# A second norm summed over all partitions, and a copy of half of retention's split outputs, in a hybrid S5 and retention layer

## The chip, the cores and the metric

The kernel runs on one core of one Trainium2 chip. The metric is the device time of one launch in microseconds (us), lower is better. A run is one timed execution; a profiled execution is one that the hardware profiler recorded, with its own time.

## The reference, cut to what matters

One decoder layer for 256 prompt positions and 8 x 8 sample positions, 320 columns together. D is 2048, the feed-forward width 5632.

```python
def rms_norm(x, g):
    y = xf * lax.rsqrt(jnp.mean(xf * xf, axis=-1, keepdims=True) + NORM_EPS)
    return (y * g.astype(jnp.float32)).astype(x.dtype)

def hybrid_layer(...):
    h = rms_norm(x, norm_mix)
    u, q, k, v, g = jnp.split(h @ w_in, [...], axis=-1)
    s5_out, s5_re, s5_im = s5_mixer(u, ...)        # scan, gelu, then y * sigmoid(y @ w_glu + b_glu)
    ...                                            # rotary, chunked retention o, group norm
    ret_out = (jax.nn.silu(g.astype(f32)) * o).astype(x.dtype)
    x = x + jnp.concatenate([s5_out, ret_out], axis=-1) @ w_out
    h2 = rms_norm(x, norm_ffn)                     # the second norm
    gate, up = jnp.split(h2 @ w_ffn_in, 2, axis=-1)
    x = x + (jax.nn.silu(gate) * up) @ w_ffn_out
    return x, s5_re, s5_im, ret_new
```

A final rms_norm follows.

## The kernel before

Everything is kept transposed: features on the 128 partitions, the 320 positions along a row. A matrix product for one block of 128 output features is a chain of products over blocks of 128 input features, into one PSUM buffer of 128x320. Each input block takes three products in fp32r (a 32-bit type of TensorE), because weights and activations are split into a high and a low part (`x = hi + lo`): hi x hi (line L143), hi x the activation's lo (L144), lo x hi (L145).

`wload` brings the weights of eight input blocks (128x1024) at a time: SP issues the transfer into `raw`, ScalarE casts to `hi` (L131), VectorE subtracts to `lo` (L133). Each of the three has a ring of three buffers, so the cast for one load waits until TensorE has done with the load three before it. Behind the first gate output the rings come from another pool (4, 3 and 3 buffers). PSUM has a ring of three accumulators (`ps_acc`).

The stages follow each other on TensorE:

1. The input projection (names ps_p), with the S5 scan and retention woven in. Retention's gated outputs, eight heads, are split by `split_r` into `r4a` (heads 0 to 3, allotted in the S5 pool `s5`) and `r4b` (heads 4 to 7).
2. The retention half of the output projection: 16 outputs of eight blocks (ps_o, L161 to L163 for outputs 0 and 1, whose halves are interleaved by `gemm_late`, then L143 to L145), evicted by an addition to `x1` on VectorE. `rhi` and `rlo` are lists of the eight split heads.
3. The GLU of S5 (ps_g, eight outputs), which reads `yhi` and `ylo`, the split of S5's output. They are allotted over the closed S5 pool; ScalarE makes `yhi` (L1087), VectorE `ylo`.
4. The S5 half of the output projection (ps_o2, shown as ps_o too, 16 outputs). Each finished block of `x1` is multiplied by the norm's weight and split into `hhi` and `hlo` for the next stage, and its square is added to `acc2`.
5. The feed-forward part: gate (ps_fg) and up (ps_fu) outputs of 16 blocks, then the down projection (ps_fo). The second norm's factor `rbc2` (128x320) is applied when a gate or up output leaves PSUM (`tt(g, pg, rbc2, MUL)`), so its sums and root may run while TensorE already works on gate output 0.

The second norm (`ffn_norm`, by `rstd_bcast`) sums `acc2` over the partitions with three products whose weights are stretches of `acc2` and whose other side is one column of ones. The sums then lie on partitions, 128x3, where VectorE takes the reciprocal root (a guess by integer arithmetic, then three Newton rounds, L174 to L190). Three more products, with an identity matrix, turn the root back into 128x320, and ScalarE copies it to `rbc2`.

What sets the order: TensorE and POOL execute in program order. Woven-in work is held by generators on a clock `clk` that counts estimated TensorE time: `spawn` with a delay, and after each block `run_due` continues what has come due; the delays are in the table `DL`. The other engines' order is set by a scheduler from dependences and priorities (`tc.high_priority`, `tc.issue_after`). Each engine then takes its queue strictly in that order. A DMA queue is filled by SP.

Of the kernel before, what the change touches and what calls it, by code (L numbers as in the profile page):

```python
# [12 lines left out]
F32 = mybir.dt.float32  # L13
F32R = mybir.dt.float32r
I32 = mybir.dt.int32
AF = mybir.ActivationFunctionType
ALU = mybir.AluOpType
ADD, SUB, MUL = ALU.add, ALU.subtract, ALU.mult
PSUM = bass.MemoryType.PSUM

P = 128
D = 2048
KT = D // P
NP, NB, NS = 256, 8, 8
N = NP + NB * NS
# [5 lines left out]
EPS = 1e-6  # L31
# [13 lines left out]
def hybrid_kernel(ctx, tc, xT, w_in, w_in4, w_out, w_glu, w_fi, w_fo, vecs, s5p, bc, x0,  # L45
# [3 lines left out]
    pe, act, dve, pool, sp = nc.tensor, nc.scalar, nc.vector, nc.gpsimd, nc.sync  # L49
# [5 lines left out]
    def f(t):  # L55
        return t.bitcast(F32)
# [13 lines left out]
    o = 0  # L70
# [8 lines left out]
    class Clk:  # L79
        now = 0.0  # L80
        n = 0
# [5 lines left out]
    def spawn(gen, delay=0.0):  # L87
        clk.n += 1
        heapq.heappush(clk.heap, (clk.now + delay, clk.n, gen))
# [11 lines left out]
    def mm(cost, *a, **k):  # L101
        pe.matmul(*a, **k)
        clk.now += cost
# [6 lines left out]
    onesr = ones.bitcast(F32R)  # L110
# [11 lines left out]
    def wload(src, nk, offset=3000):  # L122

        out = []
        with tc.high_priority(offset=offset):
            for k0 in range(0, nk, 8):
                m = min(8, nk - k0)
                raw, hi, lo = (wpool[0].tile([P, 8, P], d, name=n, tag=n, bufs=wpool[1][i])
                               for i, (n, d) in enumerate((("raw", F32), ("hi", F32R), ("lo", F32R))))
                last_raw[0] = sp.dma_start(raw[:, :m], src[:, k0:k0 + m])  # L130
                cast = act.copy(hi[:, :m], raw[:, :m])  # L131
                last_hi[0] = cast
                last_lo[0] = dve.tensor_tensor(lo[:, :m], raw[:, :m], f(hi[:, :m]), SUB)  # L133
                out += [(hi[:, i], lo[:, i]) for i in range(m)]
        return out

    def gemm(name, src, nk, xhi, xlo, ps=None, ws=None):
        ws = ws or wload(src, nk)
        if ps is None:
            pt = ps_acc.tile([P, 512], F32, name=name, tag="acc", bufs=3)  # L140
            ps = pt[:, :N]
        for k, (hi, lo) in enumerate(ws):
            pe.matmul(ps, hi, xhi[:, k], start=k == 0, stop=False)  # L143
            pe.matmul(ps, hi, xlo[:, k], start=False, stop=False)  # L144
            pe.matmul(ps, lo, xhi[:, k], start=False, stop=k == nk - 1)  # L145
            clk.now += 0.4
            if k < nk - 1:
                run_due()
        return ps

    def gemm_late(name, src, n0, ks, nk, xhi, xlo):

        ws = [wload(src(n0 + i), nk) for i in range(2)]
        pss = []
        for k0, k1 in ((0, ks), (ks, nk)):
            for i in range(2):
                if not k0:
                    pss.append(ps_acc.tile([P, 512], F32, name=name, tag="acc", bufs=3)[:, :N])
                for k in range(k0, k1):
                    hi, lo = ws[i][k]  # L160
                    pe.matmul(pss[i], hi, xhi[:, k], start=k == 0, stop=False)  # L161
                    pe.matmul(pss[i], hi, xlo[:, k], start=False, stop=False)
                    pe.matmul(pss[i], lo, xhi[:, k], start=False, stop=k == nk - 1)  # L163
                    clk.now += 0.4
                    if k < nk - 1:
                        run_due()
        return pss


    def ts(out, a, s1, o1, s2=None, o2=None):  # L170
        if o2 is None:
            dve.tensor_scalar(out, a, s1, None, o1)
        else:
            dve.tensor_scalar(out, a, s1, s2, o1, o2)  # L174
        return out

    def tt(out, a, b, op):
        dve.tensor_tensor(out, a, b, op)  # L178
        return out

    def stt(out, a, s, b, o1, o2):
        dve.scalar_tensor_tensor(out, a, s, b, o1, o2)
        return out
# [14 lines left out]
    def rstd_bcast(pool_, acc, ps_of, tag, last=None, dl=5.0, ytok=None):  # L198

        def sums(a, name):  # L200
            ps = ps_of(name)
            for i, s in enumerate(STARTS):
                mm(0.1, ps[:, i:i + 1], a[:, s:s + P], ones[:, 0:1], start=True, stop=True)
            return ps[:, 0:3]

        ms = pool_.tile([P, 3], F32, name="ms", tag=tag + "ms")
        y = pool_.tile([P, 3], F32, name="ry", tag=tag + "ry")
        if ytok is not None:
            ytok.append(y)
        tmp = pool_.tile([P, 3], F32, name="rt", tag=tag + "rt")  # L210
        ps = sums(acc, "ps_r")
        if last is not None:
            keep_warm(3)
        with tc.high_priority(offset=2000):
            ts(ms, ps, -0.5 / D, MUL, -0.5 * EPS, ADD)
            if last is not None:
                stt(ms, sums(last(), "ps_l"), -0.5 / D, ms, MUL, ADD)
            if last is not None:
                keep_warm(9)
            rsqrt(ms, y, tmp)  # L220
        yield dl
        ps2 = ps_of("ps_r2")
        for i, s in enumerate(STARTS):
            mm(0.22, ps2[:, s:s + P], y[:, i:i + 1].to_broadcast([P, P]), ident, start=True,
               stop=True)
        yield ps2[:, :N]
# [28 lines left out]
    retp = mp.tile([P, H, N], F32, name="retp")  # L255
# [652 lines left out]
    def do_g(h):  # L908
        ps = proj(11 + 4 * h)
        sg = mp.tile([P, N], F32, name="sg", tag="sg", bufs=2)  # L910
        with tc.high_priority(offset=EVAC):
# [4 lines left out]
        run_due()  # L916

    DL = dict(b1=14.2, b2=6.6, scan=17.8, y=10.0, k=8.5, v=6.1,
              o=2.2, u=6.0, c=10.0, n2=2.4, n2b=2.6, nm=0.8)
    T0, PER = 53.6, 32.0  # L920


# [11 lines left out]
    for k1 in (1, *range(2, KT + 1, 2)):  # L934
        with tc.high_priority(offset=100000), tc.manual_schedule(engines={mybir.EngineType.SP}):
# [3 lines left out]
            q = slice(k0 % 2, (k1 - 1) % 2 + 1)  # L939
# [14 lines left out]
        for k in range(k0, k1):  # L954
            for w_, x_ in ((hi, xhi), (hi, xlo), (lo, xhi)):
                for i, ps in enumerate(accs):
                    pe.matmul(ps, w_[:, k % 2, i], x_[:, k], start=k == 0 and w_ is hi and x_ is xhi,
                              stop=k == KT - 1 and w_ is lo)
# [11 lines left out]
    rg = rstd_bcast(s5, accq, misc, "n1", ytok=ytok)  # L970
# [51 lines left out]
    def advance():  # L1022
        clk.now = max(clk.now, clk.heap[0][0])
        run_due()
# [31 lines left out]

    rhi, rlo = Cols(), Cols()

    def split_r(t_, h):
        with tc.high_priority(offset=EVAC):  # L1060
            act.copy(t_[:, 0], retp[:, h])
            tt(t_[:, 1], retp[:, h], f(t_[:, 0]), SUB)
        rhi.a.append(t_[:, 0])
        rlo.a.append(t_[:, 1])

    r4a = s5.tile([P, 4, 2, N], F32R, name="r4a", tag="tab", bufs=1)
# [5 lines left out]
    rpl = rpool.enter_context(tc.tile_pool(name="rpl", bufs=1, reuse_waits="tile"))  # L1072
    r4b = rpl.tile([P, 4, 2, N], F32R, name="r4b")
    for h in range(4, H):
        while not ("sg" in HS[h] and "gn" in HS[h]):
            advance()
        split_r(r4b[:, h - 4], h)
    while clk.heap:
        advance()
    s5stack.close()  # L1080
# [8 lines left out]
    for n in range(KT):  # L1089
        if n == 0:  # L1090
            late = gemm_late("ps_o", lambda n: w_out[n, :, 8:16], 0, 4, 8, rhi, rlo)
        ps = late[n] if n < 2 else gemm("ps_o", w_out[n, :, 8:16], 8, rhi, rlo)
        tt(x1[:, n], x1[:, n], ps, ADD)
    rpool.close()
# [2 lines left out]
    for n in range(8):  # L1097
        ps = gemm("ps_g", w_glu[n], 8, yhi, ylo)
# [7 lines left out]
    hp = ctx.enter_context(tc.tile_pool(name="hp", bufs=1, reuse_waits="tile"))  # L1106
    hhi = hp.tile([P, KT, N], F32R, name="hhi")
    hlo = hp.tile([P, KT, N], F32R, name="hlo")
    acc2 = hp.tile([P, N], F32, name="acc2")
    rbc2 = hp.tile([P, N], F32, name="rbc2")  # L1110
# [6 lines left out]
    for n in range(KT):  # L1117
        if n == 0:
            late = gemm_late("ps_o2", lambda n: w_out[n, :, 0:8], 0, 6, 8, zhi, zlo)
        ps = late[n] if n < 2 else gemm("ps_o2", w_out[n, :, 0:8], 8, zhi, zlo)  # L1120
# [14 lines left out]
    fp = ctx.enter_context(tc.tile_pool(name="fp", bufs=1, side="right", reuse_waits="tile"))  # L1135
    ps_n = ctx.enter_context(tc.tile_pool(name="ps_n", bufs=2, space=PSUM))

    def norm_ps(name):
        return ps_n.tile([P, 512], F32, name=name, tag="n", bufs=2)

    def ffn_norm():
        rg = rstd_bcast(hp, acc2, norm_ps, "n2")
        next(rg)
        yield DL["n2b"]
        act.copy(rbc2, next(rg))

# [34 lines left out]
    def ffn_in(c):  # L1183
        ahi = fp.tile([P, FCT, N], F32R, name="ahi", tag="ahi", bufs=2)
        alo = fp.tile([P, FCT, N], F32R, name="alo", tag="alo", bufs=2)
        for i in range(FCT):
            n = c * FCT + i
            if n == 0:
                spawn(ffn_norm(), DL["n2"])
            pg = gemm("ps_fg", w_fi[2 * n], KT, hhi, hlo)  # L1190
            g = fp.tile([P, N], F32, name="fg", tag="fg", bufs=2)
            tt(g, pg, rbc2, MUL)
            act.activation(g, g, AF.Silu)
            if n == 0:
                wpool[:] = [wp2, WP2]
            pu = gemm("ps_fu", w_fi[2 * n + 1], KT, hhi, hlo)
            u = fp.tile([P, N], F32, name="fu", tag="fu", bufs=2)
            tt(u, pu, rbc2, MUL)
            tt(u, u, g, MUL)
            act.copy(ahi[:, i], u)  # L1200
            tt(alo[:, i], u, f(ahi[:, i]), SUB)
            if n >= 2:
                for _ in range(2 if n % 3 else 1):
                    states_step()
        return ahi, alo
# [138 lines left out]
```

## Time and profile before

| | |
|---|---|
| runs | 1433.62, 1434.41, 1434.97 us (median 1434.41) |
| profiled execution | 1433.95 us, of it 1432.1 us span |
| mean granted TensorE clock | 0.997 |
| instructions | 26209 |

The span runs from the first to the last instruction; 1.85 us lie around it. A row of the timeline has the start in us, the duration, the engine (PE is TensorE, PEld its weight loads, DVE VectorE, ACT ScalarE, SPq the transfers' queue), the source line, the operation, written tile, read tiles, shape, how many merged, and in brackets the idle time ahead of it on its engine with what ended it. Tile names lack their numbers there: `u` is `u32`, `x` is `x1`, `rbc` is `rbc2`, `acc` is `acc2`. A row of the windows has the stretch, its length, then busy time and count for PE, PEld, DVE, ACT and POOL, the granted TensorE clock, and DMA.

### The profile page before, as it was taken

How to read it: one execution, taken by the hardware profiler on the slowest of the kernel's cores; microseconds unless marked ns; L12 is line 12 of the kernel's file. 1: busy time of each engine (PE TensorE's matmuls, PEld its weight loads, DVE VectorE, ACT ScalarE, POOL GpSimd, SP SyncE). 2: the span in 40 equal slices, each digit the busy share in tenths (PEclk: the TensorE clock that was granted, in tenths of full speed). 3: DMA queues.
4: the chain of work that ended last, by engine and by line, in shares of the span. 5: the costliest groups of instructions: out<-in, count | busy, mean ns of one | idle time of the engine just before them, and what ended most of it. 6: DMA issues, size and time to landing. Idle time of an engine off the chain costs nothing.

```text
span 1432.1 us, 26209 instructions
## 1 busy us (share of the span) xinstructions
PE 1418.1 (99%) x10394; PEld 1407.6 (98%) x10394; DVE 954.6 (67%) x1853; ACT 598.8 (42%) x944; POOL 125.1 (9%) x193
## 2 busy tenths in 40 slices
PE   9999999999999999999999999999999999999996
PEld 9999999999999999999999999999999999999996
DVE  7978887777567647776677546777644767644554
ACT  7645555554355433333333333333333333333452
POOL 7530022110000010000001000001000000000001
PEclk9999999999999999999999999999999999999998
DMA  8555555556544466675666446757445765444442
GB/s 285 175 172 161 165 167 165 169 160 208 162 156 152 152 210 228 221 250 205 239 217 228 128 150 234 247 202 254 151 152 185 256 225 183 153 127 156 148 148 108
DMA packets 101803, 266.87 MB, mean 186 GB/s; under 512 B 27312, under 2 KB 41776, under 8 KB 101680
## 3 DMA queue, kind: packets, MB, share of 16 engines
q1 hardware_dynamic: 101536, 264.94, 55.7%
q8 instruction: 81, 1.33, 0.4%
q14 instruction: 42, 0.34, 0.1%
q10 hardware_dynamic: 144, 0.26, 0.1%
HBM read 254.24 MB, written 10.52 MB: 185 GB/s over the span
## 4 chain that ended last, share of the span: by engine, by line
PE 71%; DVE 1%; issue 0%; ACT 0%; DVEq 0%
PE ps_fu L144 7%; PE ps_fu L143 7%; PE ps_fo L143 7%; PE ps_fo L144 7%; PE ps_fo L145 7%; PE ps_fu L145 7%; PE ps_fg L144 7%; PE ps_fg L143 7%; PE ps_fg L145 7%; PE ps_o L145 1%; PE ps_o L143 1%; PE ps_o L144 1%; PE ps_g L144 1%; PE ps_g L145 1%; PE ps_g L143 1%; DVE x L178 0%
## 5 line engine op out<-in xcount | busy, mean ns | idle before, releaser
L131 ACT CAST hi<-raw 128x1024 fp32r<-128x1024 f32 (+1 forms) x416 | 402.2, 968 | 697.4 <-PE ps_fo L144 189.0
L133 DVE TENSOR_TENSOR lo<-raw,hi 128x1024 fp32r<-128x1024 f32 (+1 forms) x416 | 467.5, 1124 | 314.9 <-ACT hi L131 312.4
L144 PE MATMUL ps_fo<-alo,hi 128*128 128x320 f32 x704 | 217.5, 309 | 0.0
L143 PE MATMUL ps_fg<-hhi,hi 128*128 128x320 f32 x704 | 217.5, 309 | 0.0
L143 PE MATMUL ps_fo<-ahi,hi 128*128 128x320 f32 x704 | 217.5, 309 | 0.0
L145 PE MATMUL ps_fo<-ahi,lo 128*128 128x320 f32 x704 | 217.5, 309 | 0.0
L144 PE MATMUL ps_fu<-hlo,hi 128*128 128x320 f32 x704 | 217.4, 309 | 0.0
L145 PE MATMUL ps_fg<-hhi,lo 128*128 128x320 f32 x704 | 217.4, 309 | 0.0
L143 PE MATMUL ps_fu<-hhi,hi 128*128 128x320 f32 x704 | 217.4, 309 | 0.0
L144 PE MATMUL ps_fg<-hlo,hi 128*128 128x320 f32 x704 | 217.4, 309 | 0.0
L145 PE MATMUL ps_fu<-hhi,lo 128*128 128x320 f32 x704 | 217.4, 309 | 0.0
L143 PE MATMUL ps_p<-xhi,hi 128*128 128x320 f32 x560 | 177.3, 317 | 0.0
L145 PE MATMUL ps_p<-xhi,lo 128*128 128x320 f32 x560 | 173.0, 309 | 0.0
L144 PE MATMUL ps_p<-xlo,hi 128*128 128x320 f32 x560 | 172.8, 309 | 0.0
L144 PEld LDWEIGHTS ps_fg<-hlo,hi 128*128 128x128 f32 x704 | 132.4, 188 | 0.0
L143 PEld LDWEIGHTS ps_fo<-ahi,hi 128*128 128x128 f32 x704 | 132.4, 188 | 0.0
L143 PEld LDWEIGHTS ps_fu<-hhi,hi 128*128 128x128 f32 x704 | 132.4, 188 | 0.0
L144 PEld LDWEIGHTS ps_fu<-hlo,hi 128*128 128x128 f32 x704 | 132.4, 188 | 0.0
L145 PEld LDWEIGHTS ps_fo<-ahi,lo 128*128 128x128 f32 x704 | 132.4, 188 | 0.0
L145 PEld LDWEIGHTS ps_fu<-hhi,lo 128*128 128x128 f32 x704 | 132.4, 188 | 0.0
L143 PEld LDWEIGHTS ps_fg<-hhi,hi 128*128 128x128 f32 x704 | 132.3, 188 | 0.0
L145 PEld LDWEIGHTS ps_fg<-hhi,lo 128*128 128x128 f32 x704 | 132.3, 188 | 0.0
(441 smaller groups left out, 2066.6 us busy)
## 6 DMA issues: line engine op xcount, KB each, us to landing
raw<-w_fi SPq DMA_DIRECT2D x176, 512.0 KB, 4.1
raw<-w_in SPq DMA_DIRECT2D x79, 512.0 KB, 4.1
raw<-w_fo SPq DMA_DIRECT2D x64, 512.0 KB, 3.5
raw<-w_out SPq DMA_DIRECT2D x32, 512.0 KB, 3.7
hi<-vd SPq DMA_DIRECT2D x32, 512.0 KB, 5.5
lo<-vd SPq DMA_DIRECT2D x32, 512.0 KB, 5.2
raw<-w_fo SPq DMA_DIRECT2D x64, 192.0 KB, 2.4
rt<-r SPq DMA_DIRECT2D x8, 512.0 KB, 5.3
```

Source lines behind the costliest of these rows:

```text
L131: cast = act.copy(hi[:, :m], raw[:, :m])
L133: last_lo[0] = dve.tensor_tensor(lo[:, :m], raw[:, :m], f(hi[:, :m]), SUB)
L143: pe.matmul(ps, hi, xhi[:, k], start=k == 0, stop=False)
L144: pe.matmul(ps, hi, xlo[:, k], start=False, stop=False)
L145: pe.matmul(ps, lo, xhi[:, k], start=False, stop=k == nk - 1)
```

## The change

First, `r4a` is copied on ScalarE into a new tile `r4c` right behind the last `split_r`, and outputs 4 to 15 of the retention half read the copy. Second, `ffn_norm` splits `acc2` on VectorE into two fp32r parts (in tiles named fg and fu), multiplies both with a 128x128 matrix of ones, which puts the sum of every column on all partitions at once (`ps_r`, 128x320), and takes the root on 128x320 elements, straight into `rbc2`. The products with the identity and ScalarE's copy go. The sums come due 3.4 us of the clock after the first block of gate output 0.

```diff
-              o=2.2, u=6.0, c=10.0, n2=2.4, n2b=2.6, nm=0.8)
+              o=2.2, u=6.0, c=10.0, n2=3.4, nm=0.8)
...
+    last_r = [None]
     def split_r(t_, h):
         with tc.high_priority(offset=EVAC):
-            act.copy(t_[:, 0], retp[:, h])
+            last_r[0] = act.copy(t_[:, 0], retp[:, h])
...
+    r4c = rpl.tile([P, 4, 2, N], F32R, name="r4c")
+    with tc.issue_after(last_r[0].ins):
+        for q in range(2):
+            act.copy(r4c[:, 2 * q:2 * q + 2], f(r4a[:, 2 * q:2 * q + 2]))
...
     for n in range(KT):
         if n == 0:
             late = gemm_late("ps_o", lambda n: w_out[n, :, 8:16], 0, 4, 8, rhi, rlo)
+        if n == 4:
+            rhi.a[0:4], rlo.a[0:4] = ([r4c[:, h, q] for h in range(4)] for q in range(2))
...
     def ffn_norm():
-        rg = rstd_bcast(hp, acc2, norm_ps, "n2")
-        next(rg)
-        yield DL["n2b"]
-        act.copy(rbc2, next(rg))
+        shi, slo = (fp.tile([P, N], F32R, name=q, tag=q, bufs=2) for q in ("fg", "fu"))
+        ms, w = (hp.tile([P, N], F32, name=q, tag="sqx", bufs=2) for q in ("ms2", "rt2"))
+        with tc.high_priority(offset=2000):
+            dve.tensor_copy(shi, acc2)
+            tt(slo, acc2, f(shi), SUB)
+        yield DL["n2"]
+        ps = norm_ps("ps_r")[:, :N]
+        for i, a in enumerate((shi, slo)):
+            mm(0.15, ps, onesr, a, start=i == 0, stop=i == 1)
+        with tc.high_priority(offset=2000):
+            ts(ms, ps, -0.5 / D, MUL, -0.5 * EPS, ADD)
+            ts(rbc2.bitcast(I32), ms.bitcast(I32), -0.5, MUL, float(0x1EF759DF), ADD)
+            for _ in range(3):
+                tt(w, rbc2, rbc2, MUL)
+                tt(w, w, ms, MUL)
+                stt(rbc2, w, 1.5, rbc2, ADD, MUL)
...
             if n == 0:
-                spawn(ffn_norm(), DL["n2"])
+                spawn(ffn_norm())
```

How the instructions stand. On ScalarE, at the end of the retention half, before: the casts named hi_5483 and hi_5520 are for GLU outputs 0 and 1, hi_5557 for GLU output 2.

```order
L131 CAST hi_5448<-raw_5447 128x1024
L131 CAST hi_5483<-raw_5482 128x1024
L131 CAST hi_5520<-raw_5519 128x1024
L1087 ACTIVATE yhi_4949<-u32_119 128x320 x5
L131 CAST hi_5557<-raw_5556 128x1024
L1087 ACTIVATE yhi_4949<-u32_119 128x320 x3
```

After, the same instructions stand behind the last S5 chunk's GELU (y2); hi_5323 is for output 11 of the retention half, hi_5355 for output 12, hi_5387 for output 13.

```order
L693 ACTIVATE y2_4898<-y1_4897 128x320
L694 ACTIVATE y2_4898<-y2_4898,ones_69 128x320
L696 ACTIVATE y2_4898<-y2_4898 128x320
L131 CAST hi_5323<-raw_5322 128x1024
L1093 ACTIVATE yhi_4952<-u32_119 128x320 x8
L131 CAST hi_5355<-raw_5354 128x1024
L131 CAST hi_5387<-raw_5386 128x1024
```

So yhi moved from behind GLU output 1's cast to behind output 11's. On VectorE at the same place, after (lo_5324 and lo_5356 are for outputs 11 and 12; ps_o_5232, ps_o_5264 and ps_o_5296 are outputs 8, 9 and 10):

```order
L178 TENSOR_TENSOR x1_4853<-x1_4853,ps_o_5232 128x320
L133 TENSOR_TENSOR lo_5324<-raw_5322,hi_5323 128x1024
L182 SCALAR_TENSOR_TENSOR ylo_4953<-u32_119,yhi_4952 128x320 x7
L133 TENSOR_TENSOR lo_5356<-raw_5354,hi_5355 128x1024
L182 SCALAR_TENSOR_TENSOR ylo_4953<-u32_119,yhi_4952 128x320
L178 TENSOR_TENSOR x1_4853<-x1_4853,ps_o_5264 128x320
L178 TENSOR_TENSOR x1_4853<-x1_4853,ps_o_5296 128x320
```

The ylo moved there too, from behind the split of GLU output 1's weights. On ScalarE at the end of stage 1, after (hi_5067 is for output 3 of the retention half):

```order
L1063 CAST r4b_4934<-retp_110 128x320 x3
L913 ACTIVATE sg_4845<-sg_4845 128x320
L677 COPY ev_4883<-py_4858 128x320
L1063 CAST r4b_4934<-retp_110 128x320
L1083 CAST r4c_4943<-r4a_4922 128x1280 x2
L131 CAST hi_5067<-raw_5066 128x1024
```

The two copies are new there, and nothing else around them moved. On VectorE at the second norm, before; lo_6481 and lo_6487 are for the halves of up output 0, lo_6547 and lo_6553 for those of gate output 1:

```order
L178 TENSOR_TENSOR acc2_5783<-acc2_5783,sqx_6372 128x320
L174 TENSOR_SCALAR ms_6426<-ps_r_6429 128x3
...
L182 SCALAR_TENSOR_TENSOR ry_6427<-rt_6428,ry_6427 128x3
L133 TENSOR_TENSOR lo_6481<-raw_6479,hi_6480 128x1024
...
L133 TENSOR_TENSOR lo_6487<-raw_6485,hi_6486 128x1024
L133 TENSOR_TENSOR lo_6547<-raw_6545,hi_6546 128x1024
L178 TENSOR_TENSOR fg_6476<-ps_fg_6404,rbc2_5784 128x320
```

And after:

```order
L1153 CAST fg_6411<-acc2_5786 128x320
L178 TENSOR_TENSOR fu_6412<-acc2_5786,fg_6411 128x320
L133 TENSOR_TENSOR lo_6481<-raw_6479,hi_6480 128x1024
L174 TENSOR_SCALAR ms2_6413<-ps_r_6444 128x320
L133 TENSOR_TENSOR lo_6487<-raw_6485,hi_6486 128x1024
L174 TENSOR_SCALAR rbc2_5787<-ms2_6413 128x320
L178 TENSOR_TENSOR rt2_6414<-rbc2_5787 128x320
L133 TENSOR_TENSOR lo_6547<-raw_6545,hi_6546 128x1024
...
L133 TENSOR_TENSOR lo_6553<-raw_6551,hi_6552 128x1024
...
L178 TENSOR_TENSOR fg_6476<-ps_fg_6407,rbc2_5787 128x320
L178 TENSOR_TENSOR fu_6540<-ps_fu_6491,rbc2_5787 128x320
```

The splits of weights moved in between the root's operations, the first of them ahead of it; six root operations stand where the "..." ahead of lo_6553 is, and two where the one behind it is. On TensorE the sums moved from behind block 6 to behind block 9 of gate output 0, and the three products with the identity, two blocks before the end of that output, are gone. After:

```order
L144 MATMUL ps_fg_6407<-hlo_5785,hi_6402 128x320
L145 MATMUL ps_fg_6407<-hhi_5784,lo_6403 128x320
L102 MATMUL ps_r_6444<-fg_6411,ones_69 128x320
L102 MATMUL ps_r_6444<-fu_6412,ones_69 128x320
L143 MATMUL ps_fg_6407<-hhi_5784,hi_6402 128x320
```

Ahead of and behind the two products stands the same chain of gate output 0. SP's and POOL's orders are unchanged.

## The prediction

> **What bounds the kernel now.** I read the page's busy shares first, then the windows by stage, then TensorE's list of waits, and last the timeline around the two places that the change touches.
>
> ```profile
> span 1432.1 us, 26209 instructions
> PE 1418.1 (99%) x10394; PEld 1407.6 (98%) x10394; DVE 954.6 (67%) x1853; ACT 598.8 (42%) x944; POOL 125.1 (9%) x193
> ...
> 400.20:429.00 28.80, 28.47 (x195) 28.20 (x194) 18.31 (x29) 16.98 (x26) 0.00 (x0) 1.00 0.48 152
> 429.00:485.27 56.27, 56.27 (x385) 56.27 (x384) 40.33 (x63) 30.06 (x48) 0.00 (x0) 1.00 0.50 167
> 485.27:494.00 8.73, 8.68 (x63) 8.41 (x62) 5.74 (x17) 4.44 (x7) 0.00 (x0) 1.00 0.13 31
> 494.00:1416.00 922.00, 922.00 (x6288) 922.00 (x6288) 569.14 (x1065) 331.85 (x418) 26.32 (x8) 1.00 0.57 193
> ```
>
> TensorE is the bound, at a granted clock of 1.00 in each of these stretches. In the feed-forward stretch (last line) 6288 products take 922.00 us: one starts every 146.6 ns. Time is measured in these steps from here on. A product's own row lasts 309 ns and laps over the next two, so a busy TensorE can still be losing time. By steps, the second output stage (429.00 to 485.27, 16 x 8 x 3 = 384 products, 56.30 us) loses nothing, and the GLU stage (400.20 to 429.00, 192 products, 28.15 us) loses 0.65. The list of waits names the place:
>
> ```profile
> PE pss L102 <- POOL ksp L886: 0.5, 1, 0.5
> PE ps_g L144 <- DVE ylo L182: 0.3, 1, 0.3
> ```
>
> TensorE waits six times in all, by this list, and of the six only the wait on ylo lies where the change reaches. So what can be won is this wait and the steps that the norm itself takes from TensorE. VectorE and ScalarE count only where they make TensorE late.
>
> **The wait on ylo (gain).** Timeline at the start of the GLU stage:
>
> ```profile
> 397.68 1.91 ACT L1087 ACTIVATE yhi<-u 128x320 fp32r<-128x320 f32 x5
> ...
> 397.81 1.23 DVE L133 TENSOR_TENSOR lo<-raw,hi 128x1024 fp32r<-128x1024 f32 x1 [0.45 <-ACT hi L131]
> 398.95 2.09 DVE L182 SCALAR_TENSOR_TENSOR ylo<-u,yhi 128x320 fp32r<-128x320 f32 x5
> ...
> 402.39 0.31 PE L143 MATMUL ps_g<-yhi,hi 128*128 128x320 f32 x1
> 402.50 1.29 DVE L182 SCALAR_TENSOR_TENSOR ylo<-u,yhi 128x320 fp32r<-128x320 f32 x3
> ...
> 403.04 0.41 PE L144 MATMUL ps_g<-ylo,hi 128*128 128x320 f32 x1 [0.33 <-DVE ylo L182]
> ...
> 403.29 0.31 PE L145 MATMUL ps_g<-yhi,lo 128*128 128x320 f32 x1
> ```
>
> From 402.39 to 403.29 two steps should take 0.29 and take 0.90: 0.61 is lost, not the 0.33 that the wait shows. It is the order that holds them so late, not a wait: the five yhi start at 397.68 right behind a cast, with no releaser named. They are allotted over the closed S5 pool, in which r4a lies, and r4a's last reader is output 15 before and output 3 after. With the change the order puts all eight yhi behind the weights' cast for output 11, and the ylo around the split for output 12, ahead of casts that output 13 needs; ScalarE takes its queue in order, so they can't run late again. Both then lie some 18 us before their first use, and the 0.61 goes. By the rows nothing else is late there: the split at 397.81 is that of GLU output 1, wanted at 403.7, and that of output 0 lies 3.5 us ahead of it.
>
> **Where the splits of y go (cost 0).** They now stand among these rows, on ScalarE and VectorE:
>
> ```profile
> 375.63 1.05 ACT L131 CAST hi<-raw 128x1024 fp32r<-128x1024 f32 x1
> 379.15 1.05 ACT L131 CAST hi<-raw 128x1024 fp32r<-128x1024 f32 x1 [2.47 <-PE ps_o L144]
> ...
> 376.71 1.23 DVE L133 TENSOR_TENSOR lo<-raw,hi 128x1024 fp32r<-128x1024 f32 x1 [0.20 <-ACT hi L131]
> 379.30 0.49 DVE L178 TENSOR_TENSOR x<-x,ps_o 128x320 f32<-128x320 f32 x1 [1.36 <-PE ps_o L145]
> 380.23 1.23 DVE L133 TENSOR_TENSOR lo<-raw,hi 128x1024 fp32r<-128x1024 f32 x1 [0.45 <-ACT hi L131]
> ```
>
> The cast at 379.15 (output 12) is released by the end of output 9, so output 12 begins two outputs later (24 steps, 3.52 us each): 386.2. Eight yhi at 0.38 (five in 1.91) fill 376.7 to 379.8 and move that cast to 379.8, its end to 380.8. Seven ylo at 0.40 ((2.09 - 1.29)/2) run from 377.9 to 380.8, then the split for output 12 to 382.0: 4.2 us before it is needed. The eviction of output 9 (row 379.30) follows at 382.4 and ends at 382.9; its PSUM buffer is wanted by output 12, again 386.2. Both have over 3 us to spare. The issuing of transfers keeps its order on SP, and POOL's queue doesn't change.
>
> **The copies r4c (cost 0).**
>
> ```profile
> 346.26 0.46 ACT L1061 CAST r4b<-retp 128x320 fp32r<-128x320 f32 x1 [0.55 <-DVE retp L178]
> 349.25 1.05 ACT L131 CAST hi<-raw 128x1024 fp32r<-128x1024 f32 x1 [2.54 <-PE ps_o L162]
> ```
>
> No row casts 128x1280 on ScalarE. From below it costs 1.05 (128x1024). From above 1.26, along the slope between 0.46 for 320 and 1.05 for 1024 elements. Even two at 1.26 end at 349.24, inside the idle 2.54 us ahead of the next cast. If that cover were gone, the cast for output 3 would be late next: it runs at 349.25, its split is done 2.3 later, and output 3 begins at 354.5 (half of output 1 and output 2 lie between), so the copies would have to grow by 2.9 us. TensorE reads r4c from output 4 on, at 358.
>
> **The norm's products (gain).** Before, the sums and the broadcast each break into the first gate output:
>
> ```profile
> 488.21 0.31 PE L145 MATMUL ps_fg<-hhi,lo 128*128 128x320 f32 x1
> 488.36 0.72 PE L102 MATMUL ps_r<-ones,acc 128*128 128x1 f32 x6
> 488.94 0.39 PE L143 MATMUL ps_fg<-hhi,hi 128*128 128x320 f32 x1
> 489.17 0.31 PE L144 MATMUL ps_fg<-hlo,hi 128*128 128x320 f32 x1
> ...
> 491.96 0.31 PE L145 MATMUL ps_fg<-hhi,lo 128*128 128x320 f32 x1
> 492.32 0.94 PE L102 MATMUL ps_r<-ident,ry 128*128 128x128 f32 x6
> 493.01 0.39 PE L143 MATMUL ps_fg<-hhi,hi 128*128 128x320 f32 x1
> 493.24 0.30 PE L144 MATMUL ps_fg<-hlo,hi 128*128 128x320 f32 x1
> ```
>
> 488.21 to 489.17 are two ordinary steps (0.29) and 0.67 for the sums. 491.96 to 493.24 are 1.28, so 0.99 for the broadcast, a wait of some 0.2 for ry within it. Together 1.65 goes. Two products of the form 128x320 with fp32r on both sides come in. Products of that form take one step each: 0.29. From below they cost nothing (they fill no gap, so I don't take it); from above the 0.67 that the sums cost, if the change to `ones` as weights were dear. I take 0.29, since form and type are those of the neighbours. Net 1.36.
>
> The Trainium skill ("TensorE: Matmul & The Clock Gate", section "Back-to-back issue gap") gives N/2.4 + 2.5 ns for one warm product, an estimate of 136 ns at 320 columns. The rows here show 147, so the measurement decides; by the rule the pair would cost 0.27, and the whole gain would be 1.99 instead of 1.97.
>
> **The root on 320 columns, and what queues behind it (cost 0).**
>
> ```profile
> 485.27 0.31 PE L143 MATMUL ps_fg<-hhi,hi 128*128 128x320 f32 x1
> ...
> 486.83 2.92 ACT L131 CAST hi<-raw 128x1024 fp32r<-128x1024 f32 x3
> ...
> 487.06 0.48 DVE L178 TENSOR_TENSOR acc<-acc,sqx 128x320 f32<-128x320 f32 x1
> 489.12 0.16 DVE L174 TENSOR_SCALAR ms<-ps_r 128x3 f32<-128x3 f32 x1 [1.57 <-PE ps_r L102]
> ...
> 489.71 0.16 DVE L178 TENSOR_TENSOR rt<-rt,ms 128x3 f32<-128x3 f32 x1
> 489.91 0.16 DVE L182 SCALAR_TENSOR_TENSOR ry<-rt,ry 128x3 f32<-128x3 f32 x1
> ...
> 490.58 1.23 DVE L133 TENSOR_TENSOR lo<-raw,hi 128x1024 fp32r<-128x1024 f32 x1
> ...
> 492.54 2.36 DVE L133 TENSOR_TENSOR lo<-raw,hi 128x1024 fp32r<-128x1024 f32 x2 [0.27 <-issue]
> 494.81 0.48 DVE L178 TENSOR_TENSOR fg<-ps_fg,rbc 128x320 f32<-128x320 f32 x1
> ```
>
> On VectorE an operation of 320 columns lasts 0.48, and one that needs its predecessor starts 0.04 after it ends (0.16 long, 0.20 apart above): I take 0.52 each, between 0.20 (three columns) and 0.52. Times stay on the old axis; all of it shifts by the 0.61 alike. The two halves of acc2 run from 487.6 to 488.6. TensorE comes to the sums after 30 products, at 485.27 + 30 x 0.1466 = 489.67, so it doesn't wait. The first lo then runs in the idle time that stood ahead of ms, two microseconds earlier than before. The sums are there at 490.12 and ms starts at 490.16. Behind it stand, in this order: lo for the second half of "up" output 0, two root operations, lo for gate output 1, six root operations, lo for its second half, two more, then the eviction.
>
> | needed by TensorE | from | ready at |
> |---|---|---|
> | second half of up 0 | 492.60 + 3.52 = 496.1 | 490.16 + 0.52 + 1.23 = 491.9 |
> | gate 1 | 499.6 | 494.1 |
> | its second half | 503.2 | 498.4: its cast waits for the weights' buffer (496.1), then 1.05 and 1.23 |
> | gate 0's PSUM buffer (for up 1) | 506.7 | 500.0: two root operations and the eviction |
>
> The eviction moves from 494.81 to about 499.5, and nobody waits for it before 506.7. The copy of rbc2 on ScalarE goes (off the path); the casts that now stand ahead of the first SiLU wait for TensorE's buffers, and SiLU's result is used only in the down projection.
>
> The Trainium skill ("VectorE: DVE Perf Modes", section "The DRAIN you can't avoid") has the next operation start only when the pipe is empty. The dependent rows agree (0.20 apart for 0.16), the independent ylo don't (0.40 apart). By that rule this longer chain, eleven operations, is a cost; it would be one only beyond the point of the third rival.
>
> **Sum.** 0.61 + 1.65 - 0.29 = 1.97 off the profiled execution, which took 1433.95 (span 1432.1 and 1.85 around it) and lies 0.46 under the median of 1434.41: 1431.98 there, 1432.4 as a median.
>
> **Rivals.** A change of 0.2% (2.87 us) is about what a measurement of this kernel can tell from none.
> 1. The products wait for the split of acc2. Against it: 1.1 us to spare. If cast and subtraction took three times 0.52 (no row shows VectorE casting 320 columns), TensorE would stand 1.0: 1433.5. Chance 0.08.
> 2. The early splits of y win nothing, because another operand, a weights' split say, keeps the GLU stage's start late. Against it: the split at 397.81 has 4.7 us to spare. Only the norm's 1.36 stays: 1433.0. Chance 0.07.
> 3. Slower: the root starves the weights. Nine root operations and two lo (2.4) stand ahead of lo for gate 1's second half, which must start by 501.9; 490.16 + 9p + 2.4 passes that at p = 1.04 us an operation. Slower by over 0.2% needs 4.84 lost against my forecast, p = 1.58, three times the rows: 1437.5. Chance 0.05.
> 4. Faster by over 0.2%: the pair costs nothing (2.26 gained, 1432.15) and the runs fall as far under it as the lowest shown does under its median (0.79): 1431.4. No third place in the list of waits speaks for more. Chance 0.12.
>
> **Numbers.** My forecast has 0.68: 1432.4. The range goes from rival 4 (1431.4, and 0.2 below it) to rival 1 with the upper scatter of the runs (1433.5 + 0.56, so 1434.1), which leaves out rival 3 and the outer part of 1 and 4. Faster 0.12, same 0.83 (0.68 + 0.08 + 0.07), slower 0.05.
>
> **What would show it.** In the profile after, TensorE's list has no wait of ps_g on ylo, and the GLU stage takes 28.2. yhi x8 stands near 376, and its weights' casts keep their 3.5 us beat by output 13. r4c ends by 349.3. In the first gate output the pair sits between ordinary steps with 0.29 in all, with no second break. The root's steps are about 0.5, rbc2 is ready near 499, and "up" 0 and gate 1 start without a wait. I am wrong if TensorE waits for lo or fu in that stretch, or if a new wait appears between outputs 9 and 13.

## The result, and the profile after

| | before | after |
|---|---|---|
| median of 22 runs each, on the same chip | 1434.19 us (1432.99 to 1436.07) | 1432.24 us (1431.32 to 1433.81) |
| profiled execution | 1433.95, span 1432.1 | 1432.50, span 1430.7 |

The ratio is 0.9987, with a 95% interval of 0.9982 to 0.9993. That is 1.9 us less (1.0 to 2.6), under the 0.2% named as what the measurement can tell, where 1.97 was forecast. With this many runs the interval still leaves out a ratio of 1. That the two medians lie 1.95 apart, so near the forecast, is luck within this interval; the stages below carry the reading. Of the later kernels' runs, two of the ten of rounds6 took 2420.61 and 7948.32 us: they are in its median but not in its ratio.

First the page after, the windows of the stages that correspond to those shown before (their bounds moved with the stages), and the whole of TensorE's list of waits:

```profile
span 1430.7 us, 26192 instructions
PE 1415.7 (99%) x10384; PEld 1405.6 (98%) x10384; DVE 959.7 (67%) x1855; ACT 600.5 (42%) x945; POOL 123.7 (9%) x193
...
400.75:428.92 28.17, 28.17 (x195) 28.17 (x194) 16.41 (x23) 15.88 (x23) 0.00 (x0) 1.00 0.49 157
428.92:485.23 56.31, 56.31 (x387) 56.31 (x385) 40.35 (x63) 30.06 (x48) 0.00 (x0) 1.00 0.49 167
```

```profile
PE pss L102 <- POOL ksp L886: 1.4, 1, 1.4
PE warm_ps L116 <- POOL ones L62: 1.1, 1, 1.1
PE py L102 <- DMA toe<-toe: 0.7, 1, 0.7
PE py L957 <- DVE xhi L178: 0.5, 1, 0.5
PE pst L107 <- ACT kd L730: 0.3, 1, 0.3
PE py L957 <- DVE xlo L277: 0.2, 1, 0.2
PE py L957 <- ACT hi L947: 0.2, 1, 0.2
```

The GLU stage now runs from 400.75 to 428.92, 28.17 against 28.15 for 192 bare steps; before it lost 0.65. The wait of ps_g on ylo is gone from the list. What is left there lies in stage 1, and it is not the same from one execution to the next: the wait on ksp is 0.5 in one profile and 1.4 in the other, though nothing changed there. So the two spans cannot be subtracted as they stand. I count from two marks on TensorE, the first product of the GLU stage and the first of gate output 0. This is the timeline of after at both (before they stand at 400.19 and 485.27):

```profile
400.75 0.31 PE L143 MATMUL ps_g<-yhi,hi 128*128 128x320 f32 x1
400.89 0.31 PE L144 MATMUL ps_g<-ylo,hi 128*128 128x320 f32 x1
...
485.23 0.31 PE L143 MATMUL ps_fg<-hhi,hi 128*128 128x320 f32 x1
```

From the GLU mark to the gate mark: 85.08 before, 84.48 after. From the gate mark to the span's end: 946.83 before (1432.1 - 485.27), 945.47 after. The first piece holds the wait on ylo, the second the norm. They give 0.60 and 1.36, together 1.96.

The second norm in the timeline after, TensorE's rows first, then VectorE's (acc is acc2, and fg and fu are here the two parts of acc2):

```profile
489.63 0.31 PE L102 MATMUL ps_r<-fg,ones 128*128 128x320 f32 x1
489.78 0.31 PE L102 MATMUL ps_r<-fu,ones 128*128 128x320 f32 x1
489.93 0.31 PE L143 MATMUL ps_fg<-hhi,hi 128*128 128x320 f32 x1
```

```profile
487.53 0.33 DVE L1153 CAST fg<-acc 128x320 fp32r<-128x320 f32 x1
487.97 0.49 DVE L178 TENSOR_TENSOR fu<-acc,fg 128x320 fp32r<-128x320 f32 x1
...
490.12 0.49 DVE L174 TENSOR_SCALAR ms<-ps_r 128x320 f32<-128x320 f32 x1 [0.53 <-PE ps_r L102]
...
498.89 0.49 DVE L182 SCALAR_TENSOR_TENSOR rbc<-rt,rbc 128x320 f32<-128x320 f32 x1
499.41 0.49 DVE L178 TENSOR_TENSOR fg<-ps_fg,rbc 128x320 f32<-128x320 f32 x1
```

The pair takes 489.63 to 489.93, two ordinary steps, and nothing breaks the stream a second time. The parts of acc2 are done at 488.46, 1.2 ahead of the pair. The root ends at 499.38 and the eviction at 499.90, some 6.7 ahead of the 506.65 at which "up" output 1 takes its PSUM buffer.

### The profile page after: what moved, and what is told of

The parts are those of the page before. It is cut to its first block, busy times and chain, and to the rows that moved or that the text cites. A ratio compares the mean times of both kernels' runs of the same rounds, so it can differ in the third digit from the quotient of the medians.

```text
span 1430.7 us, 26192 instructions
## 1 busy us (share of the span) xinstructions
PE 1415.7 (99%) x10384; PEld 1405.6 (98%) x10384; DVE 959.7 (67%) x1855; ACT 600.5 (42%) x945; POOL 123.7 (9%) x193
## 4 chain that ended last, share of the span: by engine, by line
PE 75%; DVE 1%; DMA 0%; issue 0%; ACT 0%; SPq 0%; DVEq 0%; ACTq 0%
PE ps_fo L143 7%; PE ps_fg L144 7%; PE ps_fu L144 7%; PE ps_fo L145 7%; PE ps_fg L145 7%; PE ps_fu L145 7%; PE ps_fu L143 7%; PE ps_fg L143 7%; PE ps_fo L144 7%; PE ps_o L144 2%; PE ps_o L143 2%; PE ps_o L145 2%; PE ps_g L144 1%; PE ps_g L145 1%; PE ps_g L143 1%; PE ps_o L161 0%
## 5 line engine op out<-in xcount | busy, mean ns | idle before, releaser
L144 PEld LDWEIGHTS ps_fo<-alo,hi 128*128 128x128 f32 x704 | 132.4, 188 | 0.0
```

## The experiments

Nine kernels, each compared with the kernel before on the same chip. In the table, times are from the profile, one of each kernel; the run ratios carry their 95% intervals, and effects under 1 us lie within them. The two columns of stages don't scatter: where nothing is changed they repeat to 0.06, with spans that are given to 0.1.

| kernel | GLU mark to gate mark | gate mark to end | median, ratio to before |
|---|---|---|---|
| before | 85.08 | 946.83 | |
| after | 84.48 | 945.47 | 1432.24, 0.9987 (0.9982 to 0.9993) |
| copy_only | 84.49 | 946.86 | 1434.32, 0.9997 (0.9988 to 1.0005) |
| norm_only | 85.09 | 945.48 | 1433.20, 0.9990 (0.9981 to 0.9999) |
| reader15 | 84.48 | 945.49 | 1432.57, 0.9988 (0.9979 to 0.9997) |
| six_ahead | 84.48 | 945.53 | 1433.99, 0.9996 (0.9986 to 1.0005) |
| early_sums | 84.48 | 947.85 | 1435.59, 1.0007 (0.9998 to 1.0016) |
| rounds6 | 84.48 | 945.73 | 1433.11, 0.9989 (0.9979 to 0.9999) |
| rounds8 | 84.48 | 951.43 | 1438.59, 1.0033 (1.0020 to 1.0046) |
| rounds9 | 84.48 | 953.99 | 1440.74, 1.0046 (1.0029 to 1.0062) |
| rounds12 | 84.48 | 958.89 | 1445.99, 1.0079 (1.0066 to 1.0093) |

### The two halves of the change, each alone

copy_only is the changed kernel with the old norm (its two delays and its `spawn` with a delay come back too):

```diff
-        shi, slo = ...          # split of acc2, products with ones, root on 128x320
...
+        rg = rstd_bcast(hp, acc2, norm_ps, "n2")
+        next(rg)
+        yield DL["n2b"]
+        act.copy(rbc2, next(rg))
```

> Edit: the copy r4c stays, the second norm is the old one again. My theory, two TensorE losses that have nothing to do with each other: only the 0.61 us wait on ylo goes. The list of waits has no ps_g on ylo, the GLU stage has even steps of 0.147, but the first gate output keeps its two breaks (0.67 and 0.99). From the first product of ps_g to the span's end: 1031.91 before, 1029.95 in the changed kernel, 1031.3 here; as a time 0.6 under the kernel before, which the runs alone can't tell from nothing (ratio 0.9996, give or take 0.0005). Rival A, the copy carries the whole gain (the early splits shift everything behind them): 1029.95 here. Rival B, the norm alone carries it and the wait would have gone anyway: 1031.9, with a wait of ps_g on ylo or on another operand.

norm_only is the kernel before with the new norm (r4c is not made, all outputs read r4a):

```diff
-    r4c = rpl.tile([P, 4, 2, N], F32R, name="r4c")
...
-        if n == 4:
-            rhi.a[0:4], rlo.a[0:4] = ...
```

> Edit: the new norm stays, the copy r4c goes, all 16 outputs of the retention half read r4a. My theory: the 0.61 us wait of ps_g on ylo stands again and yhi stands behind the cast for GLU output 1; the old norm's two breaks (1.65) are gone and the pair takes 0.29. From the first product of ps_g to the span's end 1031.91 - 1.36 = 1030.55; as a time 1.4 under the kernel before (ratio 0.9991). Rival A, the copy carries the whole gain: 1031.9. Rival B, the norm carries it all: 1029.95. Rival C, what the norm wins is lost again downstream, since the root holds VectorE for longer: between 1030.6 and 1031.9, with a wait of TensorE on lo or on an evicted buffer behind 494 us.

From the GLU mark to the end copy_only took 1031.35 and norm_only 1030.57, within 0.05 of what my theory gave. The gains add up: 0.59 in copy_only's first column and 1.35 in norm_only's second, 1.96 in the changed kernel. In copy_only the norm's two breaks stand as before:

```profile
489.02 0.72 PE L102 MATMUL ps_r<-ones,acc 128*128 128x1 f32 x6
...
492.99 0.93 PE L102 MATMUL ps_r<-ident,ry 128*128 128x128 f32 x6
```

In norm_only the old order of ScalarE and the old wait stand again (timelines of ScalarE and TensorE; yhi stands right behind the cast of GLU output 1):

```profile
398.32 1.91 ACT L1087 ACTIVATE yhi<-u 128x320 fp32r<-128x320 f32 x5
```

```profile
403.03 0.31 PE L143 MATMUL ps_g<-yhi,hi 128*128 128x320 f32 x1
403.68 0.42 PE L144 MATMUL ps_g<-ylo,hi 128*128 128x320 f32 x1 [0.34 <-DVE ylo L182]
```

So the rivals in which one half carries all fall, and neither half gives back what the other wins.

### What sets the place of y's splits

reader15 lets only the last output read the copy:

```diff
-        if n == 4:
+        if n == 15:
             rhi.a[0:4], rlo.a[0:4] = ([r4c[:, h, q] for h in range(4)] for q in range(2))
```

> Edit: only output 15 reads the copy r4c, outputs 0 to 14 read r4a. It asks what sets the place of y's splits. My theory: the order follows r4a's last reader, so yhi stands behind the cast for GLU output 0, one weights' cast earlier than in the kernel before, and most of ylo with it; that is one output (3.5 us) earlier, and the wait of 0.61 is over by then. The list has no ps_g on ylo; from the first product of ps_g to the span's end 1029.95, as in the changed kernel. Rival A: 12 outputs' distance is needed, because ylo has to stand ahead of the splits of GLU outputs 0 and 1: the wait stays, 1030.55. Rival B, the copy helps by keeping TensorE's reads apart from ScalarE's or VectorE's traffic and not by the order: a part of the 0.61 stays, in proportion to the outputs that read r4a.

It took 1029.97 from the GLU mark. Its ScalarE and VectorE rows show the last splits of y only one cast earlier than in the kernel before, far from output 11:

```profile
397.72 1.19 ACT L1093 ACTIVATE yhi<-u 128x320 fp32r<-128x320 f32 x3
```

```profile
399.02 1.29 DVE L182 SCALAR_TENSOR_TENSOR ylo<-u,yhi 128x320 fp32r<-128x320 f32 x3
```

The last ylo ends at 400.31, as the stage begins at 400.23, and the products that read it come later. The order follows r4a's last reader (output 14 here), and one output's distance wins as much as twelve. A benefit in proportion to the outputs that read the copy is excluded: eleven of the twelve went back to r4a and all of the 0.60 stayed. Whether yhi could be put earlier without any copy was not tried.

### The cover of the copies taken away

six_ahead makes the copies three times over and puts all six ahead of the casts (the values are the same):

```diff
-    with tc.issue_after(last_r[0].ins):
-        for q in range(2):
+    with tc.issue_after(last_r[0].ins), tc.high_priority(offset=5000):
+        for q in (0, 1) * 3:
             act.copy(r4c[:, 2 * q:2 * q + 2], f(r4a[:, 2 * q:2 * q + 2]))
```

> Edit: the copies to r4c are made three times over (six instructions instead of two, the same values), with a priority that puts all six ahead of the weights' cast for output 3. This takes the copies' cover away. My theory: six at 1.20 from 346.98 end at 354.2 on the changed kernel's axis; the cast for output 3 runs to 355.2 and its split to 356.5; output 3 starts at 354.99 and wants its lo with the third product at 355.28. TensorE waits there, first on hi and then on lo, about 1.2 in all (1.0 to 1.5), once. From the first product of ps_o to the first of ps_g: 56.42 in the changed kernel, 57.6 here; from there to the end 1029.95 as before. Rival: ScalarE makes it up, because the weights' buffers of output 3 have slack that I did not see: 56.4, no wait on hi or lo.

Timelines of ScalarE, VectorE and TensorE:

```profile
348.01 7.06 ACT L1083 CAST r4c<-r4a 128x1280 fp32r<-128x1280 f32 x6
354.97 2.94 ACT L131 CAST hi<-raw 128x1024 fp32r<-128x1024 f32 x3
```

```profile
357.33 0.41 PE L145 MATMUL ps_o<-r4a,lo 128*128 128x320 f32 x1 [0.70 <-DVE lo L133]
```

From the first product of ps_o (345.12) to the GLU mark (402.89) it took 57.77, against 56.42 in the changed kernel: 1.35 lost where 1.2 was expected, on lo of output 3 as said. Counted from the first product of ps_o, the cast for output 3 starts 4.41 later than in the changed kernel (9.85 against 5.44). There its split is done at 352.07 and first read by output 3's third product at 355.28, so the room was 3.21; the prediction had 2.9, counted to the first product. That leaves 1.20, as expected; the rest is TensorE's start behind the split and its longer first step (357.33 to 357.58). So the copies cost nothing because ScalarE stands idle there, and not because copies are cheap.

### The cover of the products taken away

early_sums lets the pair come due early, which is rival 1 made to happen:

```diff
-               ... n2=3.4, nm=0.8)
+               ... n2=0.4, nm=0.8)
```

> Edit: the delay of the pair of products is 0.4 instead of 3.4, so they stand behind block 1 of gate output 0 (6 products) instead of block 9 (30 products); nothing else changes. This is my first rival's mechanism, made to happen. My theory: TensorE comes to the pair at 0.9 us into the output; the second half of acc2's split is ready 3.3 us into it (in the changed kernel 488.4 against 485.9 for the output's first product), so TensorE stands about 2.4 (2.2 to 2.7) and the list of waits has ps_r on fu (or on fg) with it. From the first product of ps_g to the span's end 1029.95 + 2.4 = 1032.4, slower than the kernel before by 0.4. Rival: TensorE has work ahead in the weight loads or VectorE is not yet late, so that less than 1 is lost: 1030.9 or less.

```profile
486.08 0.31 PE L145 MATMUL ps_fg<-hhi,lo 128*128 128x320 f32 x1
488.13 0.38 PE L102 MATMUL ps_r<-fg,ones 128*128 128x320 f32 x1 [1.74 <-DVE fg L1153]
488.63 0.42 PE L102 MATMUL ps_r<-fu,ones 128*128 128x320 f32 x1
488.89 0.30 PE L143 MATMUL ps_fg<-hhi,hi 128*128 128x320 f32 x1
```

From 486.08 to 488.89 three steps should take 0.44 and take 2.81. 2.37 is lost, and the gate mark to the end grew by 2.38: nothing made it up. The gain depends on the pair's place in TensorE's order; eight blocks earlier, the norm's whole gain of 1.36 is gone and a microsecond more.

### The cover of the root taken away

These change one number, the count of Newton rounds (3 in the changed kernel), first to 6 and 12:

```diff
-            for _ in range(3):
+            for _ in range(6):
```

> Edit: the root takes 6 Newton rounds instead of 3, 20 operations of 128x320 on VectorE instead of 11; the added rounds refine a value that no longer changes. This sits at the point where the root's cover ends. My theory: nine more operations at 0.52 (4.7) and the splits that the order puts between them move the end of gate output 0's eviction from 499.9 to about 506.9; up output 1 wants the PSUM buffer at 506.6, so TensorE loses about 0.25 (0 to 0.6), and no weights are late. From the first product of ps_g to the span's end 1029.95 + 0.25 = 1030.2. Rival A, weights late (my third rival's form): a wait on lo between 496 and 506 and a loss over 1. Rival B, the cover is larger: no loss and no wait on an eviction there.

> Edit: the root takes 12 Newton rounds instead of 3, so 38 operations of 128x320 on VectorE instead of 11; the added rounds refine a value that no longer changes. This takes the cover of the root away. My theory: the chain goes on at 0.52 per operation with the weights' splits in between. The splits for up output 0 and gate output 1 stand where VectorE gets to them in time, so no weights are late; the eviction of gate output 0 ends near 517.4 on the changed kernel's axis, its PSUM buffer is wanted by up output 1 at 506.6, and TensorE waits there about 10.8 (10 to 12). From the first product of ps_g to the span's end 1029.95 + 10.8 = 1040.8, ratio to the kernel before about 1.006. Rival A, my third rival as I put it: a split of weights is late first, and TensorE waits for lo of gate output 1's second half. Rival B: VectorE works the rounds off in idle time and little is lost, under 3.

With 6 rounds 0.26 was lost, by the marks. VectorE's and TensorE's rows show the eviction ending at 506.10, when TensorE had wanted its buffer at 506.09 (505.94 and a step):

```profile
505.61 0.49 DVE L178 TENSOR_TENSOR fg<-ps_fg,rbc 128x320 f32<-128x320 f32 x1
```

```profile
505.94 0.31 PE L145 MATMUL ps_fg<-hhi,lo 128*128 128x320 f32 x1
506.25 0.39 PE L143 MATMUL ps_fu<-hhi,hi 128*128 128x320 f32 x1
```

That 0.25 was expected is in part luck. On the changed kernel's axis (0.56 later) the eviction ends at 506.66 and not at 506.9, so by my reckoning hardly anything would be lost. What I had left out made up for it: TensorE started 0.15 behind the eviction's end, and its first step behind the stop was 0.22 long.

With 12 rounds the wait came where it was expected, on the eviction (fg), not on a weights' split, but 13.42 was lost and not 10.8. TensorE's rows and the windows around them (granted clock third from the right in the windows):

```profile
518.69 0.61 PE L143 MATMUL ps_fu<-hhi,hi 128*128 128x320 f32 x1 [11.20 <-DVE fg L178]
519.09 0.47 PE L144 MATMUL ps_fu<-hlo,hi 128*128 128x320 f32 x1
519.36 0.47 PE L145 MATMUL ps_fu<-hhi,lo 128*128 128x320 f32 x1
```

```profile
509.00:510.00 1.00, 0.00 (x0) 0.00 (x0) 1.00 (x2) 0.72 (x1) 0.00 (x0) 0.70 0.94 365
...
523.00:524.00 1.00, 1.00 (x9) 1.00 (x8) 0.00 (x0) 0.00 (x0) 0.00 (x0) 0.98 0.00 0
```

The product ahead of the wait started at 507.18, so one step later TensorE was free: it stood from 507.33 to 518.69, 11.36. Behind the wait products start 0.27 apart instead of 0.147, 16 of them until 523.08, which takes 4.39 instead of 2.35: 2.04 more. Together 13.40. My number lacked the second loss and had the wait 0.6 too short. Most of that 0.6 comes from one operation of the root on VectorE, 1.21 long where the others take 0.49:

```profile
512.60 1.21 DVE L178 TENSOR_TENSOR rt<-rbc 128x320 f32<-128x320 f32 x1
```

POOL began an operation of 2.81 us at 512.40; whether that is the cause stays open. Two more kernels ask whether that second loss grows with the wait; they have 8 and 9 rounds.

> Edit: the root takes 8 Newton rounds instead of 3 (26 operations on VectorE); the added rounds refine a value that no longer changes. Open is why 12 rounds cost 13.4 where 10.8 was expected: TensorE stood 11.4 and then ran its next 16 products at half the granted clock, 2.0 more. My theory: the clock falls when TensorE has stood for some microseconds, and that second loss is then nearly fixed. By VectorE's rows of the runs with 6 and 12 rounds, the eviction of gate output 0 ends 4.2 later than with 6 rounds (six operations at 0.525 and one split more ahead of it), so TensorE stands 4.4. From the first product of ps_g to the span's end 1029.95 + 4.4 = 1034.35 if the clock holds, 1036.4 if it falls as with 12 rounds. Early sums stood 1.9 and kept a clock of 1.00, so I take it that somewhere between 1.9 and 11.4 it falls; I expect a fall here, 0.6. Rival: the clock falls with the length of the wait in proportion, so that a wait of 4.4 costs some 0.8 more, 1035.1. The Trainium skill (TensorE: Matmul & The Clock Gate, the part on the clock gate) has half the rate after an idle window of about 3.4 us that runs freely and the same time to come back; by that the fall here depends on where the window lies.

> Edit: the root takes 9 Newton rounds instead of 3 (29 operations on VectorE); the added rounds refine a value that no longer changes. Three more operations than with 8 rounds and no split more: TensorE stands 4.4 + 1.6 = 6.0. My theory, a second loss that is nearly fixed: the granted clock is 0.50 for some 4 us behind the wait and 2.0 is lost on top, so from the first product of ps_g to the span's end 1029.95 + 6.0 + 2.0 = 1037.95 (1037 to 1038.2). Rival A, in proportion to the wait: 1.1 on top, 1037.0. Rival B, the clock holds until far longer waits: 1035.95.

With 8 rounds TensorE stood 4.33 and lost 5.96, so 1.6 more than the wait (1035.91 from the GLU mark, between the 1035.1 of the rival and the 1036.4 expected); with 9 rounds it stood 5.90 and lost 8.52, 2.6 more, which is outside the 1037 to 1038.2 that I gave (1038.47 from the GLU mark). The second loss is there at a wait of 4.3 and does not grow with it (1.6, 2.6, 2.0 for 4.3, 5.9, 11.4), but it isn't fixed either. A clock that holds is excluded, and a loss in proportion as well. The section on the hardware says what sets it.

## Why the prediction was right, point by point

- **The wait on ylo, 0.61.** Right: 0.60 by the marks, alone and together with the norm. ScalarE has no idle time ahead of yhi in either kernel, so what held the splits late was their place in its order; reader15 shows that this place follows r4a's last reader.
- **Where the splits of y go, cost 0.** Right. ScalarE and VectorE after, with all times later by the 0.55 of stage 1:

```profile
377.12 2.99 ACT L1093 ACTIVATE yhi<-u 128x320 fp32r<-128x320 f32 x8
380.01 1.04 ACT L131 CAST hi<-raw 128x1024 fp32r<-128x1024 f32 x1
383.20 1.05 ACT L131 CAST hi<-raw 128x1024 fp32r<-128x1024 f32 x1 [2.15 <-PE ps_o L144]
386.72 1.05 ACT L131 CAST hi<-raw 128x1024 fp32r<-128x1024 f32 x1 [2.46 <-PE ps_o L144]
```

```profile
378.38 2.90 DVE L182 SCALAR_TENSOR_TENSOR ylo<-u,yhi 128x320 fp32r<-128x320 f32 x7
381.20 1.22 DVE L133 TENSOR_TENSOR lo<-raw,hi 128x1024 fp32r<-128x1024 f32 x1
```

  The cast for output 12 starts at 380.01 (379.8 was said on the old axis), its split ends at 382.42, over 4 us before output 12, and by output 13's cast at 383.20 the beat of 3.5 us is back. No wait of TensorE lies there.
- **The copies, cost 0.** Right: the two end at 349.40, and the next cast keeps its start (349.77, which is 349.25 with the shift). Each lasts 1.26, which is the upper bound; the second starts 1.16 behind the first, so that both take 2.42.

```profile
346.98 2.42 ACT L1083 CAST r4c<-r4a 128x1280 fp32r<-128x1280 f32 x2
349.77 1.05 ACT L131 CAST hi<-raw 128x1024 fp32r<-128x1024 f32 x1 [0.37 <-PE ps_o L162]
```

- **The norm's products, 1.65 less 0.29.** Right: 1.36 by the marks and by norm_only. The pair costs two steps of 0.15 and not nothing, so rival 4's premise fell.
- **The root, cost 0.** Right in its sum and in its step of 0.52. Two of the new operations have one source and are shorter than the 0.48 taken: the cast of acc2 takes 0.33, above, and the integer guess 0.32. The eviction's move to "about 499.5" is measured as 499.41. The prediction set the ylo rows, 0.40 apart, against the Trainium skill ("VectorE: DVE Perf Modes", section "The DRAIN you can't avoid"); the same section adds that a next operation which is not held starts earlier, so they are no evidence against it.
- **Rival 1** was right as a mechanism (early_sums), with its cover of 1.1 measured as 1.2. **Rival 2** fell: the early splits win the whole 0.60.
- **Rival 3's** named victim was wrong, for a root made longer by more operations: with 6, 8, 9 and 12 rounds it is the eviction of gate output 0 that is late, never lo of gate output 1, because the order puts the splits between the rounds. The point from which it costs was in my table as the PSUM buffer, with 6.7 to spare; six rounds use it up. Operations that are each slower, the rival's own form, were not tried. Its price was also linear, and a wait of 4 us costs nearly 6 here; by its own terms (1432.4 + 4.84) it is 1437.2 and not 1437.5.

## What to carry to other kernels

Where one engine is full, count what an edit takes out of its stream and what it puts in, in that engine's own steps, and for all other work look only for the buffer that is wanted first. Then two numbers are needed for each covered piece, its room and who is late when the room is gone; here the pieces had 1.2 (the pair), 3.2 (the copies) and 6.7 us (the root), and each was confirmed by using it up. To measure effects that are smaller than the scatter of whole runs, set two marks on the full engine behind the place where the scatter arises: here the marks repeat to 0.06 us while 22 runs of each kernel left the gain between 1.0 and 2.6.

## What the hardware showed that was not expected

The granted clock falls during a long stop of TensorE or just behind it, and it falls and comes back in a fixed grid. With 8 rounds (windows) it falls at 512.12 (0.56 is the mean of 0.12 at 1.00 and 0.88 at 0.50) and is back at 515.52; the stop had ended at 511.92:

```profile
512.00:513.00 1.00, 1.00 (x5) 1.00 (x6) 0.96 (x3) 0.68 (x3) 0.27 (x1) 0.56 1.09 410
...
515.00:516.00 1.00, 1.00 (x7) 1.00 (x6) 0.00 (x0) 0.00 (x0) 0.61 (x1) 0.74 0.10 37
```

The same reading of the 9 rounds' rows

```profile
511.00:511.50 0.50, 0.00 (x0) 0.00 (x0) 0.47 (x2) 0.00 (x0) 0.00 (x0) 0.69 1.02 393
...
518.00:519.00 1.00, 1.00 (x9) 1.00 (x8) 0.00 (x0) 0.35 (x1) 0.00 (x0) 0.99 0.00 0
```

gives 511.19 and 518.02, and of the 12 rounds' rows above 509.40 and 523.04. The clock is low for 3.40, 6.83 and 13.64: once, twice and four times 3.41. I read it as windows of 3.41 us that don't start with the stop. A window counts as idle even when TensorE worked in part of it: with 12 rounds it stood for only the last 2.07 of the 3.41 before the fall. An idle time of 1.25 in a window was let pass (9 rounds, the window that ended at 507.78). So was early_sums' stop of 1.90, but that one lay across a border of the grid, which can be counted back from the clock's fall at the end of its span (1426.42):

```profile
1426.00:1427.00 1.00, 0.00 (x0) 0.00 (x0) 1.00 (x3) 0.00 (x0) 1.00 (x2) 0.71 0.57 223
```

With 12 rounds 268 windows fit between 523.04 and the fall at the end, 1437.82, so a window is 3.4133 long, and 275 of them ahead of 1426.42 a border lies at 487.76. The stop, from 486.23 to 488.13, put 1.53 into one window and 0.37 into the next. By this reading a stop of 2.1 us that lies in one window already lowers the clock; no run here tried that.

To bring the clock back takes more work: with 9 rounds the window from 511.19 to 514.60, idle for its first 1.24 and busy from 512.43 on, did not do it. A window need not be busy throughout, though. At the start of six_ahead's span products start 0.27 apart until 6.58 and 0.15 apart soon behind, so the clock rose there, although TensorE had waited 0.48 in the 3.41 before:

```profile
5.38 0.61 PE L957 MATMUL py<-xhi,hi 128*128 128x320 f32 x1 [0.48 <-DVE xhi L178]
...
6.58 0.33 PE L957 MATMUL py<-xlo,hi 128*128 128x320 f32 x1
```

What is lost on top of a stop is the work done at the low clock: with 8, 9 and 12 rounds TensorE worked 3.40, 5.59 and 4.35 us at steps of 0.27 in place of 0.147, which makes 1.5, 2.5 and 2.0 of the measured 1.6, 2.6 and 2.0. So early_sums' stop cost its own length, and those from 4.3 on cost 1.6 to 2.6 more, by where the grid lies.

The Trainium skill ("TensorE: Matmul & The Clock Gate", section "What's actually happening") states a free-running window of 3413 ns and half the clock after at least one idle window. The length and the grid agree with these runs; an idle window, taken as one without any work, does not, by the 2.07 of 12 rounds.

The other thing is where the scatter sits: the GLU mark lay between 400.19 and 401.69 in the ten profiles other than six_ahead, with stage 1 nearly the same in all of them, and from there on the time repeats. What moves the waits of stage 1 (ksp 0.5 to 1.5) stays open.
